# Products by seven in an FFN: which units use them, and where VectorE's differences stand

## The chip, the cores and the metric

The kernel runs on one core of a Trainium2 chip. The metric is the device time of one execution in microseconds, the median of several runs.

## The reference

One decoder block on 256 tokens of width 2048, in float32: two SwiGLU networks around a mixing layer and a cross-attention, each added to the stream h.

```python
h = h + 0.5 * swiglu(rms_norm(h, ffn1_norm), w_gate, w_up, w_down)   # FFN 1: 2048 -> 5632 -> 2048
n = rms_norm(h, mix_norm); P = n @ w_in                              # retention (8 heads) and
h = h + concat(ret, swa) @ w_out                                     # sliding-window attention (16 heads)
h = h + memory_cross_attention(rms_norm(h), rms_norm(mem))           # 4 heads, 256 memory tokens
h = h + 0.5 * swiglu(rms_norm(h, ffn2_norm), ...)                    # FFN 2
out = rms_norm(h, final_norm)
def swiglu(x, w_gate, w_up, w_down):
    return (silu(x @ w_gate) * (x @ w_up)) @ w_down
```

## The kernel before

**A product.** Float32 accuracy is made from three products: each operand is kept as a high part (a rounded copy, made by ScalarE) and a low part (the rest, made by VectorE), and `three` (L664) multiplies high by high, high by low and low by high. The activations stand on the stationary side, 128 tokens at a time; the weights stream in 512 columns. A weight tile `wf` of 128 x 1024 (512 KB) is loaded by a DMA of SyncE's queue into a ring of 11 places, then split: `wh` by ScalarE (L81), `wl` by VectorE (L391), each in a ring of 4. One such tile feeds one step: 2 pieces of the contraction x 2 token halves x 3 = 12 products of 512 columns.

**Units and twins.** A `Unit` is one matrix times 512 columns: 4 blocks of the contraction x 2 steps. A `Twin` joins two matrices (gate and up of the same 512 columns, or two column blocks of a down matrix). Some of its blocks are plain, 4 steps each. A block in `sevens` is done by Strassen's scheme in Winograd's form: 7 half-size products take the place of 8. Each is a chunk, of a kind P1 to P7, with 6 products of 512 columns; so a block costs 42 instead of 48. A chunk's weights are a loaded tile (P1, P3, P5, P2) or a difference of tiles, which `difference` (L244) makes on VectorE in place: P5 is u0 - g0, P6 is u1 - u0, P7 is u1 - g0, P4 is g1 - u1. On the other side stand sums of the activations (`sums_of`, `sums_into` at L302). Each chunk's weights are split like any tile. A chunk's result is combined with the others by copies on ScalarE and additions on VectorE (L265). A unit with two blocks in `sevens` is called here a unit with two groups.

**Order of the work.** FFN units are numbered b = 0 to 10 (512 of the 5632 columns each), in three groups (0 to 3, 4 to 7, 8 to 10); after each group the down product of that group runs. `all_steps` writes one list of steps; the first chunks (P1, P3, P5, P6, P7) of a twin with `ahead` are spread over the steps of the unit before it, P2 and P4 over its own. `run_stream` walks this list: weights are loaded 8 steps and split 3 steps ahead of their products, and `later(n, fn)` issues a task n steps on. The order so written is given to a scheduler, which sets each engine's queue by the data that each instruction needs; tasks keep their place by an explicit dependence (`order`), splits and differences need not. So a difference can stand in VectorE's queue well ahead of the place where it was written.

**Around it.** `cross` (L638) turns a result's layout: VectorE transposes, ScalarE's queue writes to DRAM (`box`), GpSimd's queue reads it back into `t4k`, and a task some steps later (`TURN` = 6 and more) uses it. `Norm.finish` sums the squares of the norm (L593 on VectorE, L596 on TensorE: two products with a column of ones, shown in the profile as four passes) and computes the scale; it is issued `delay` steps after the last square. For the first norm, `n1`, this is early in FFN 1. Twins take their four PSUM banks in turn from two pools, `tmp` (with `spare`) and `acc`. In FFN 1 all units from b = 1 on are twins, with block 2 by seven, and with blocks 2 and 3 for b = 4 and 8 (`DOUBLE`). In FFN 2 it is block 0, and blocks 0 and 1 for b = 4 and 8.

In the mixing stage `rqk_done` rotates q and k (L959 to L963) and `ret_scores` (L972) multiplies them.

Of the kernel before, what the change touches and what calls it, by code (L numbers as in the profile page):

```python
# [43 lines left out]
def decoder_block(ctx: ExitStack, tc: tile.TileContext, a: dict, out: bass.AP):  # L44
# [68 lines left out]
    def later(delay, fn):  # L113
        tasks.append((clock[0] + delay, len(tasks), fn))
# [74 lines left out]
    class Twin:  # L189
# [23 lines left out]
            return self.plain[len(self.plain) - self.late :]  # L213

        def chunks(self, kinds):
            return [
                (self, c, None, kind, c == self.sevens[0], c == self.sevens[-1]) for kind in kinds for c in self.sevens
            ]

        def steps(self):  # L220
            return [
# [16 lines left out]
        def difference(self, b, kind):  # L238
            if kind not in (P5, P6, P7, P4) or (b, kind) in self.made:
                return  # L240
            self.made.add((b, kind))
            g0, g1, u0, u1 = (self.tiles.get((b, f, half)) for f in range(2) for half in range(2))
            dst, p, q = {P5: (u0, u0, g0), P6: (u1, u1, u0), P7: (g0, u1, g0), P4: (u1, g1, u1)}[kind]
            nc.vector.tensor_tensor(dst, p, q, ALU.subtract)  # L244

        def prepare(self, b, kind, between):
            self.difference(b, kind)
# [61 lines left out]
    def sums_of(norm, b, dst, delay, src=None):  # L309

        y = [None]
        src = hT[b] if src is None else src

        def scale():
            y[0] = blk(F32).rearrange("p k c s -> p (k c s)")
            x = y[0][:, :1024].rearrange("p (j k s) -> p j k s", j=2, k=2)
            for k in range(4):
                g = norm.gcol + 4 * b + k
                copy(x[:, k % 2, k // 2, :], src[:, k, :], scale=gains[:, g : g + 1])

        def add():
            x = y[0][:, :1024].rearrange("p (j k s) -> p j k s", j=2, k=2)
            y.append(y[0][:, 1024:].rearrange("p (i j s) -> p i j s", i=4, j=2))
            sums_into(y[1], lambda t, k: x[:, :, k, t * P : (t + 1) * P])

        def part():
            dst[b] = split_sums(y[1])
        for i, fn in enumerate((scale, add, part)):
            later(delay + i, fn)
# [337 lines left out]
    def to_h(w, lhs, factor, blocks, norm=None, then=None, spare=0, seven=None, sums=None, plain=0):  # L667

        def done(s, b):
            if factor != 1.0:  # L670
                y = [t2k() for _ in s]
                for i in range(2):
                    copy(y[i], s[i], scale=factor)
                s = y

            def add(out):
                for t in range(2):
                    v = hT[b][:, :, t * P : (t + 1) * P].rearrange("p q (a j) -> p q a j", a=4)
                    nc.vector.tensor_tensor(v, v, out[t], ALU.add)  # L679
                if norm is not None:  # L680
                    norm.block(b, [hT[b]])
                    norm.stat([hT[b]])
                if then is not None:
                    then(b)
            cross(s, add, TURN + (1 + b // 2 if norm is nmix else spare))
        for b in range(4):
            if seven is None or b < plain:
                Unit(w, b, 512, lhs, lambda acc, b=b: done(acc, b), blocks, pair=True)
            elif b % 2 == 0:
                twin(  # L690
                    [w[2 * i : 2 * i + 2] for i in (b, b + 1)], lhs, [x for x in blocks if x != seven], [seven], sums,
                    lambda f, s, b=b: done(s, b + f),
                )

    twins, input_sums = [], {}

    def twin(*args):

        twins.append(Twin(*args, ahead=bool(twins), spare=len(twins) % 2 == 0))

    def ffn(norm, w_gate, w_up, down, groups, turned):
        gated = {}
        made = {}
        acts = {}

        def gate_done(b, acc):
            assert norm.ready
            gated[b] = [t2k() for _ in range(2)]
            for t in range(2):
                nc.scalar.activation(gated[b][t], acc[t], AF.Silu, scale=norm.scale(t))  # L710

        def up_done(b, acc):
            s = gated.pop(b)
            for t in range(2):
                nc.vector.scalar_tensor_tensor(s[t], acc[t], norm.scale(t), s[t], ALU.mult, ALU.mult)
            turn(b, s)

        def both_done(b, f, acc):
            (gate_done, up_done)[f](b, acc)

        def turn(b, s):

            def made(out):
                acts[b] = blk()
                halves_of(out, parts_of(acts[b]))
                if b in starts:
                    y = blk(F32).rearrange("p k c s -> p (k c s)")[:, :1024].rearrange("p (i j s) -> p i j s", i=4, j=2)
                    sums_into(y, lambda t, k: out[t][:, 2 * k : 2 * k + 2])
                    asums[b] = split_sums(y)
            cross(s, made, TURN + (3 if b < 10 else 1))  # L730

        sums, asums = {}, {}
        twins.clear()
        input_sums[norm] = sums
        starts = [x[0] for x in groups]
        for g, fbs in enumerate(groups):
            for b in fbs:
                done = functools.partial(both_done, b)
                if b > 0:
                    sevens = turned[: 1 + (b in DOUBLE)]  # L740
                    plain = [x for x in range(4) if x not in sevens]
                    twin([w[2 * b : 2 * b + 2] for w in (w_gate, w_up)], norm.blocks, plain, sevens, sums, done)
                    if b == 1:
                        norm.bank = functools.partial(twins[0].bank, 0, 1)
                    continue
                for f, w in enumerate((w_gate, w_up)):
                    Unit(w, b, 512, norm.blocks, functools.partial(done, f), range(4), pair=True)
                if norm is not n1:
                    together(2)
            down(g, acts, fbs, asums)  # L750

# [2 lines left out]
    for b in range(4):  # L754
        if b > 0:
            later(4 * b - 1, lambda b=b: n1.block(b, [hT[b]]))
        later(4 * b + 2 * (b < 3), lambda b=b: n1.stat([hT[b]]))
    for at, b in ((8, 2), (40, 3)):
        later(at, lambda b=b: sums_of(n1, b, input_sums[n1], 0))

    def load_x(b, lo, hi):
        nc.sync.dma_start(hT[b][:, lo:hi, :], a["x"][b * P : (b + 1) * P, lo:hi, :])

    later(24, lambda: nc.sync.dma_start(sinks, a["sinks"]))

    nmix = Norm(G_MIX, "nmix", 3, spread=True)

    def near_mix(b):
        if b == 0:
# [10 lines left out]
            to_h(a["ffn1_w_down"], acts, 0.5, fbs, nmix, near_mix, seven=fbs[0], sums=sums)  # L780
            units[-2].rest = 4

    ffn(n1, a["ffn1_w_gate"], a["ffn1_w_up"], ffn1_down, (range(0, 4), range(4, 8), range(8, 11)), (2, 3))

# [156 lines left out]
    def rqk_done(g, which):  # L943
        def done(acc):
            def finish(out):
                if "rot" not in st:
                    st["rot"] = st["ctab"][:, C_COSR : C_COSR + 512].rearrange("p (c s) -> p c s", c=2)
                    nmix.spread_over(st["rot"])
                if which == 0:
                    st["qk"] = blk(F32)  # L950
                qk = st["qk"]
                for t in range(2):
                    x = out[t]
                    cos, sin = (
                        st["rot"][:, c, t * P : (t + 1) * P].rearrange("p (o a j) -> p o a j", o=1, a=4)
                        .broadcast_to([P, 4, 4, 32]) for c in range(2)
                    )
                    r = squares_of(t2k())
                    nc.vector.tensor_tensor(r[:64], x[64:], sin[64:], ALU.mult)  # L959
                    nc.vector.tensor_tensor(r[64:], x[:64], sin[:64], ALU.mult)  # L960
                    nc.vector.tensor_tensor(x, x, cos, ALU.mult)
                    dst = qk[:, :, which, t * P : (t + 1) * P].rearrange("p q (a j) -> p q a j", a=4)
                    nc.vector.tensor_tensor(dst, x, r, ALU.add)  # L963
                if which == 1:
                    for i in range(4):
                        later(3 + i // 2, lambda i=i: ret_scores(g, i, qk))
            cross(acc, finish, TURN + 2)
        return done

    def ret_scores(g, i, qk):  # L970
        ps = tmp_ps()
        nc.tensor.matmul(ps[:, :S], qk[:, i, 1, :P], qk[:, i, 0, :], start=True, stop=True)  # L972
        nc.tensor.matmul(ps[:, S : S + P], qk[:, i, 1, P:], qk[:, i, 0, P:], start=True, stop=True)
        sT = t2k()
        dm = st["dmat"][g][:, i * S : (i + 1) * S]
        nc.vector.tensor_tensor(sT[:, :S], ps[:, :S], dm, ALU.mult)
        nc.vector.tensor_tensor(sT[:, S : S + P], ps[:, S : S + P], dm[:, :P], ALU.mult)
        st["sT", g, i] = sT
# [375 lines left out]
```

## Time and profile before

| | |
|---|---|
| median of 3 runs | 2144.3 us (2142.32 to 2144.52) |
| the profiled execution | 2140.22 us, of which the span of instructions is 2138.3 us |
| TensorE products busy | 2119.8 us (99%) |
| VectorE busy | 1698.5 us (79%) |
| ScalarE busy | 1236.2 us (58%) |
| GpSimd busy | 161.6 us (8%) |
| DMA | 482.61 MB, 226 GB/s on average |
| TensorE's granted clock, mean | 0.997 |

PE is TensorE's products and PEld its weight loads, DVE is VectorE, ACT ScalarE, POOL GpSimd, SP SyncE. A row of a timeline has the start (us from the span's start), the duration, engine, line, operation and tiles, the count of merged instructions, and in brackets the idle time before it and what ended that. Tile numbers are left out in profiles. A row of a group has the count, the busy time, the mean duration in ns, and the engine's idle time just before these instructions.

### The profile page before, as it was taken

How to read it: one execution, taken by the hardware profiler on the slowest of the kernel's cores; microseconds unless marked ns; L12 is line 12 of the kernel's file. 1: busy time of each engine (PE TensorE's matmuls, PEld its weight loads, DVE VectorE, ACT ScalarE, POOL GpSimd, SP SyncE). 2: the span in 40 equal slices, each digit the busy share in tenths (PEclk: the TensorE clock that was granted, in tenths of full speed). 3: DMA queues.
4: the chain of work that ended last, by engine and by line, in shares of the span. 5: the costliest groups of instructions: out<-in, count | busy, mean ns of one | idle time of the engine just before them, and what ended most of it. 6: DMA issues, size and time to landing. Idle time of an engine off the chain costs nothing.

```text
span 2138.3 us, 26847 instructions
## 1 busy us (share of the span) xinstructions
PE 2119.8 (99%) x9564; PEld 1754.4 (82%) x9564; DVE 1698.5 (79%) x1997; ACT 1236.2 (58%) x1549; POOL 161.6 (8%) x273
## 2 busy tenths in 40 slices
PE   9999999999999999999999999999999999999998
PEld 7888788887888888878888888888888888888886
DVE  7887898778888788777887566578888888888875
ACT  6665565555666664546566454456666556555654
POOL 0000000000100210100101110011010000000000
PEclk9999999999999999999999999999999999999999
DMA  8677787777877876667878875586887677766773
GB/s 301 210 238 217 216 262 235 221 218 220 274 223 233 266 215 203 207 200 241 242 230 234 260 226 186 163 270 216 250 249 244 195 225 218 234 198 208 225 241 113
DMA packets 221286, 482.61 MB, mean 226 GB/s; under 512 B 18144, under 2 KB 18144, under 8 KB 221152
## 3 DMA queue, kind: packets, MB, share of 16 engines
q1 hardware_dynamic: 191312, 413.72, 61.6%
q0 software_dynamic: 12288, 33.57, 7.0%
q10 hardware_dynamic: 17552, 33.60, 4.3%
q8 instruction: 75, 1.23, 0.3%
q14 instruction: 59, 0.48, 0.1%
HBM read 445.17 MB, written 35.65 MB: 225 GB/s over the span
## 4 chain that ended last, share of the span: by engine, by line
PE 89%; DVE 5%; DMA 3%; issue 1%; ACT 1%; POOL 0%; DVEq 0%; ACTq 0%; POOLq 0%; SPq 0%
PE acc L664 55%; PE tmp L664 33%; DVE wl L391 2%; DMA wf<-in_ffn_w_up 1%; DMA wf<-in_ffn_w_gate 1%; DMA wf<-in_xa_wk 1%; ACT wh L81 1%; DVE blk L547 0%; DMA t4k<-box 0%; DMA wf<-in_ffn_w_down 0%; DVE t2k L585 0%; DVE h L679 0%; ACT blk L81 0%; DMA box<-t4k 0%; PE tmp L898 0%
## 5 line engine op out<-in xcount | busy, mean ns | idle before, releaser
L81 ACT ACTIVATE wh<-wf 128x1024 fp32r<-128x1024 f32 (+1 forms) x891 | 933.9, 1054 | 733.5 <-PE acc L664 416.6
L391 DVE TENSOR_TENSOR wl<-wf,wh 128x1024 fp32r<-128x1024 f32 (+1 forms) x886 | 1069.0, 1218 | 349.5 <-ACT wh L81 332.6
L664 PE MATMUL acc<-wh,blk 128*128 128x512 f32 (+1 forms) x3840 | 1211.8, 388 | 1.6 <-ACT wh L81 1.0
L664 PEld LDWEIGHTS acc<-wh,blk 128*128 128x128 f32 x3840 | 719.7, 188 | 151.4 <-ACT wh L81 2.0
L664 PE MATMUL acc<-wl,blk 128*128 128x512 f32 (+1 forms) x1920 | 744.5, 388 | 0.3 <-DVE wl L391 0.3
L664 PE MATMUL tmp<-wh,blk 128*128 128x512 f32 x2232 | 716.7, 390 | 0.0
L664 PEld LDWEIGHTS tmp<-wh,blk 128*128 128x128 f32 x2232 | 419.5, 188 | 87.5 <-ACT t2k L81 0.3
L664 PE MATMUL tmp<-wl,blk 128*128 128x512 f32 x1116 | 435.1, 390 | 2.5 <-DVE wl L391 2.5
L664 PEld LDWEIGHTS acc<-wl,blk 128*128 128x128 f32 x1920 | 361.8, 188 | 73.6 <-DVE wl L391 1.7
L647 POOL DMA_DIRECT2D t4k<-box x256 | 147.8, 584 | 1743.5 <-ACT wh L81 420.3
L664 PEld LDWEIGHTS tmp<-wl,blk 128*128 128x128 f32 x1116 | 209.8, 188 | 47.7 <-DVE wl L391 4.2
L244 DVE TENSOR_TENSOR wf<-wf,wf 128x1024 f32<-128x1024 f32 x152 | 185.9, 1223 | 31.3 <-DMA wf<-in_ffn_w_up 18.5
L81 ACT ACTIVATE t2k<-tmp 128x512 f32<-128x512 f32 x88 | 52.5, 597 | 33.6 <-PE tmp L664 21.1
L638 DVE STREAM_TRANSPOSE t4k<-t2k 128x512 f32<-128x512 f32 x96 | 64.5, 695 | 5.9 <-ACT t2k L81 5.5
L81 ACT ACTIVATE t2k<-acc 128x512 f32<-128x512 f32 x76 | 45.1, 596 | 29.7 <-PE acc L664 15.4
L86 DVE TENSOR_TENSOR blk<-t4k,blk 128x512 fp32r<-128x512 f32 (+2 forms) x72 | 44.3, 655 | 1.3 <-ACT blk L81 0.9
L81 ACT ACTIVATE blk<-t4k 128x512 fp32r<-128x512 f32 (+2 forms) x72 | 39.6, 595 | 3.3 <-DMA t4k<-box 2.6
L81 ACT ACTIVATE blk<-h,gains 128x256 fp32r<-128x256 f32 (+1 forms) x80 | 34.2, 496 | 11.6 <-DVE h L679 9.9
L265 DVE TENSOR_TENSOR tmp<-t2k,tmp 128x512 f32<-128x512 f32 x54 | 35.6, 690 | 0.0
L265 DVE TENSOR_TENSOR acc<-t2k,acc 128x512 f32<-128x512 f32 x48 | 31.7, 689 | 0.0
L547 DVE SCALAR_TENSOR_TENSOR blk<-h,gains,blk 128x256 fp32r<-128x256 f32 x64 | 26.8, 479 | 3.9 <-ACT blk L81 3.7
L679 DVE TENSOR_TENSOR h<-h,t4k 128x512 f32<-128x512 f32 x40 | 25.7, 684 | 2.7 <-DMA t4k<-box 2.7
(141 smaller groups left out, 607.7 us busy)
## 6 DMA issues: line engine op xcount, KB each, us to landing
wf<-in_ffn_w_gate SPq DMA_DIRECT2D x176, 512.0 KB, 5.1
wf<-in_ffn_w_up SPq DMA_DIRECT2D x176, 512.0 KB, 5.0
wf<-in_ffn_w_down SPq DMA_DIRECT2D x176, 512.0 KB, 4.6
box<-t4k ACTq DMA_DIRECT2D x64, 512.0 KB, 5.4
t4k<-box POOLq DMA_DIRECT2D x256, 128.0 KB, 7.1
wf<-in_w_in_rqk SPq DMA_DIRECT2D x32, 512.0 KB, 4.7
wf<-in_w_in_rvg SPq DMA_DIRECT2D x32, 512.0 KB, 4.7
wf<-in_w_out SPq DMA_DIRECT2D x32, 512.0 KB, 5.0
```

Of the source, the lines that this page charges most:

```text
L81: return nc.scalar.activation(dst, src, AF.Copy, **kw)
L86: nc.vector.tensor_tensor(lo, src, hi, ALU.subtract)
L244: nc.vector.tensor_tensor(dst, p, q, ALU.subtract)
L265: nc.vector.tensor_tensor(out, a, b, ALU.add)
L391: nc.vector.tensor_tensor(lo[:, cs], wf[:, cs], hi[:, cs], ALU.subtract)
L547: nc.vector.scalar_tensor_tensor(x[:, k, 1, :], v[:, k, :], g, x[:, k, 0, :], ALU.mult, ALU.subtract)
L638: nc.vector.transpose(z[:, t, :].rearrange("p (g q j) -> p q g j", g=4, q=4), squares_of(v))
L647: nc.gpsimd.dma_start(z[32 * g : 32 * g + 32].rearrange("p t (i n) -> p (t i) n", i=4), far[g])
L664: nc.tensor.matmul(o, x, y, start=first, stop=last, skip_group_check=shared)
L679: nc.vector.tensor_tensor(v, v, out[t], ALU.add)
```

## The change

The parts are these. A difference is tied to the instruction of VectorE that was written just before it, so it can't move ahead of that. In FFN 1 the second unit (b = 1) becomes two plain units, gate and up, and b = 4 and 8 have one group, so only block 2 is ever done by seven, and the sums of block 3 are gone; those of block 2 are made later. In a twin with two groups, which FFN 2 keeps, the chunks of one group come before those of the other, P7 of both last. `ahead` and `spare` are handed over where the count of twins no longer gives what it did. The second norm's statistic is issued one step later, the rotation of q and k one step earlier, with the scores at the same step as before.

```diff
         def chunks(self, kinds):
-            return [
-                (self, c, None, kind, c == self.sevens[0], c == self.sevens[-1]) for kind in kinds for c in self.sevens
-            ]
+            pairs = [(kind, c) for c in self.sevens for kind in kinds if kind != P7]
+            pairs += [(P7, c) for c in self.sevens if P7 in kinds]
+            return [(self, c, None, kind, c == self.sevens[0], c == self.sevens[-1]) for kind, c in pairs]
...
+            last = look()[mybir.EngineType.DVE]
             nc.vector.tensor_tensor(dst, p, q, ALU.subtract)
+            order(last, look()[mybir.EngineType.DVE])
...
-                    lambda f, s, b=b: done(s, b + f),
+                    lambda f, s, b=b: done(s, b + f), **({"spare": True} if plain else {}),
...
-    def twin(*args):
-
-        twins.append(Twin(*args, ahead=bool(twins), spare=len(twins) % 2 == 0))
+    def twin(*args, **kw):
+
+        twins.append(Twin(*args, **{"ahead": bool(twins), "spare": len(twins) % 2 == 0, **kw}))
...
-                if b > 0:
-                    sevens = turned[: 1 + (b in DOUBLE)]
+                if b > (norm is n1):
+                    sevens = turned if b in DOUBLE else turned[:1]
                     plain = [x for x in range(4) if x not in sevens]
-                    twin([w[2 * b : 2 * b + 2] for w in (w_gate, w_up)], norm.blocks, plain, sevens, sums, done)
+                    twin(
+                        [w[2 * b : 2 * b + 2] for w in (w_gate, w_up)], norm.blocks, plain, sevens, sums, done,
+                        ahead=b > 1,
+                    )
...
-                if norm is not n1:
+                if norm is not n1 or b == 1:
                     together(2)
...
-    for at, b in ((8, 2), (40, 3)):
-        later(at, lambda b=b: sums_of(n1, b, input_sums[n1], 0))
+    later(19, lambda: sums_of(n1, 2, input_sums[n1], 0))
...
-    nmix = Norm(G_MIX, "nmix", 3, spread=True)
+    nmix = Norm(G_MIX, "nmix", 4, spread=True)
...
-    ffn(n1, a["ffn1_w_gate"], a["ffn1_w_up"], ffn1_down, (range(0, 4), range(4, 8), range(8, 11)), (2, 3))
+    ffn(n1, a["ffn1_w_gate"], a["ffn1_w_up"], ffn1_down, (range(0, 4), range(4, 8), range(8, 11)), (2,))
...
-                        later(3 + i // 2, lambda i=i: ret_scores(g, i, qk))
-            cross(acc, finish, TURN + 2)
+                        later(4 + i // 2, lambda i=i: ret_scores(g, i, qk))
+            cross(acc, finish, TURN + 1)
```

In the changed kernel some lines have new numbers: L244 (difference) is L245, L391 (split) L393, L593 L595, L596 L598, L598 L600, L664 (product) L666, L679 L681.

What this does to the engines' queues is seen at two places. The first is the statistic of the first norm. VectorE's queue before, in the rows that end with the sum of squares (L593, L598): the `wl` are splits, L547 and L585 the low parts and squares of block 3, L244 a difference of unit 1.

```order
L391 TENSOR_TENSOR wl_59_408<-wf_57_405,wh_58_407 128x1024
L547 SCALAR_TENSOR_TENSOR blk_60_423<-h3_78,gains_79,blk_60_423 128x256 x4
L391 TENSOR_TENSOR wl_63_435<-wf_61_432,wh_62_434 128x1024
L585 TENSOR_TENSOR t2k_24_216<-t2k_24_216,t2k_64_450 128x512
L391 TENSOR_TENSOR wl_68_459<-wf_66_456,wh_67_458 128x1024
L585 TENSOR_TENSOR t2k_24_216<-t2k_24_216,t2k_65_453 128x512
L391 TENSOR_TENSOR wl_78_482<-wf_69_462,wh_77_481 128x1024
L244 TENSOR_TENSOR wf_61_432<-wf_61_432,wf_69_462 128x2x2x256
L391 TENSOR_TENSOR wl_80_498<-wf_70_464,wh_79_497 128x1024
L593 TENSOR_TENSOR t2k_24_216<-t2k_24_216 128x256
L391 TENSOR_TENSOR wl_84_517<-wf_61_432,wh_83_516 128x1024
L598 TENSOR_SCALAR ms_82_513<-tmp_73_469 128x2
```

And VectorE's queue now, at the same place:

```order
L393 TENSOR_TENSOR wl_61_423<-wf_59_420,wh_60_422 128x1024
L587 TENSOR_TENSOR t2k_24_216<-t2k_24_216,t2k_62_438 128x512
L587 TENSOR_TENSOR t2k_24_216<-t2k_24_216,t2k_63_441 128x512
L393 TENSOR_TENSOR wl_66_447<-wf_64_444,wh_65_446 128x1024
L393 TENSOR_TENSOR wl_72_471<-wf_67_450,wh_71_470 128x1024
L595 TENSOR_TENSOR t2k_24_216<-t2k_24_216 128x256
L600 TENSOR_SCALAR ms_75_492<-tmp_74_489 128x2
```

Two splits stand between the last square and the sum (L595), and no difference. On TensorE the two products with ones stood here before, 153 products of 512 columns after the first two steps (11 whole steps of 12, 9 of the next, and two chunks of 6):

```order
L664 MATMUL acc_29_228<-wh_67_458,blk_60_423 128x512
L664 MATMUL acc_29_228<-wl_68_459,blk_60_423 128x512
L664 MATMUL acc_29_228<-wh_67_458,blk_60_423 128x512
L596 MATMUL tmp_73_469<-ones_91,t2k_24_216 128x1 x2
L664 MATMUL acc_29_228<-wh_67_458,blk_60_423 128x512
L664 MATMUL acc_29_228<-wl_68_459,blk_60_423 128x512
```

And now, after 145 of them (12 whole steps and 1 of the next):

```order
L666 MATMUL acc_29_228<-wl_57_396,blk_58_411 128x512
L666 MATMUL acc_29_228<-wh_56_395,blk_58_411 128x512
L666 MATMUL acc_20_160<-wh_60_422,blk_58_411 128x512
L598 MATMUL tmp_74_489<-ones_91,t2k_24_216 128x1 x2
L666 MATMUL acc_20_160<-wl_61_423,blk_58_411 128x512
L666 MATMUL acc_20_160<-wh_60_422,blk_58_411 128x512 x2
```

The last split ahead of the sum (`wl_72`) takes the places of a step whose products end 13 products before this one.

The second place is VectorE's queue in the down product of FFN 1's first group, where unit 4 is prepared. Before, with L679 the addition of a down result to h:

```order
L244 TENSOR_TENSOR wf_407_2097<-wf_407_2097,wf_374_1950 128x2x2x256
L391 TENSOR_TENSOR wl_390_2030<-wf_374_1950,wh_389_2029 128x1024
L391 TENSOR_TENSOR wl_393_2048<-wf_381_1982,wh_392_2047 128x1024
L391 TENSOR_TENSOR wl_396_2060<-wf_385_1998,wh_395_2059 128x1024
L244 TENSOR_TENSOR wf_414_2131<-wf_414_2131,wf_385_1998 128x2x2x256
L391 TENSOR_TENSOR wl_399_2078<-wf_388_2016,wh_398_2077 128x1024
L391 TENSOR_TENSOR wl_406_2094<-wf_391_2033,wh_405_2093 128x1024
L244 TENSOR_TENSOR wf_391_2033<-wf_391_2033,wf_407_2097 128x2x2x256
L244 TENSOR_TENSOR wf_374_1950<-wf_391_2033,wf_374_1950 128x2x2x256
L391 TENSOR_TENSOR wl_409_2112<-wf_394_2051,wh_408_2111 128x1024
L679 TENSOR_TENSOR h0_75<-h0_75,t4k_364_1910 128x4x128 x2
L391 TENSOR_TENSOR wl_413_2128<-wf_397_2063,wh_412_2127 128x1024
```

And now:

```order
L393 TENSOR_TENSOR wl_391_2063<-wf_380_2000,wh_390_2062 128x1024
L681 TENSOR_TENSOR h0_75<-h0_75,t4k_353_1877 128x4x128 x2
L393 TENSOR_TENSOR wl_394_2083<-wf_383_2018,wh_393_2082 128x1024
L245 TENSOR_TENSOR wf_389_2048<-wf_389_2048,wf_374_1965 128x2x2x256
L393 TENSOR_TENSOR wl_402_2101<-wf_386_2036,wh_401_2100 128x1024
L393 TENSOR_TENSOR wl_404_2118<-wf_389_2048,wh_403_2117 128x1024
L681 TENSOR_TENSOR h1_76<-h1_76,t4k_366_1935 128x4x128 x2
L393 TENSOR_TENSOR wl_407_2138<-wf_392_2066,wh_406_2137 128x1024
L245 TENSOR_TENSOR wf_383_2018<-wf_383_2018,wf_389_2048 128x2x2x256
L393 TENSOR_TENSOR wl_410_2150<-wf_395_2086,wh_409_2149 128x1024
L393 TENSOR_TENSOR wl_412_2167<-wf_383_2018,wh_411_2166 128x1024
```

Before, the differences in `wf_407` and `wf_414` each stand 13 rows ahead of the splits that read them, which lie past the rows shown, and two differences follow each other; now each stands two rows ahead of its split (`wf_389` and `wl_404`, `wf_383` and `wl_412`). FFN 2's differences move in the same way.

## The prediction

> **What bounds the kernel now.** I read the page's first part, then the stretches of equal length, then TensorE's waits, and only then the rows around each wait. The first fence has the busy times and TensorE's waits (us in total, times, longest); the second has stretches of 50 us: length, busy time of PE, PEld, DVE, ACT and POOL with instructions in brackets, granted clock, DMA share, GB/s.
>
> ```profile
> PE 2119.8 (99%) x9564; PEld 1754.4 (82%) x9564; DVE 1698.5 (79%) x1997; ACT 1236.2 (58%) x1549; POOL 161.6 (8%) x273
> ...
> PE tmp L596 <- DVE t2k L593: 3.5, 3, 2.2
> PE tmp L664 <- DVE wl L391: 2.5, 4, 0.9
> PE tmp L972 <- DVE blk L963: 0.8, 2, 0.5
> PE acc L664 <- ACT t2k L81: 0.6, 1, 0.6
> ```
>
> ```profile
> 0.00:50.00 50.00, 45.91 (x215) 39.04 (x215) 37.41 (x56) 34.83 (x56) 0.70 (x6) 1.00 0.84 306
> 50.00:100.00 50.00, 49.58 (x206) 40.69 (x207) 40.72 (x45) 28.74 (x34) 4.09 (x5) 0.93 0.69 207
> 100.00:150.00 50.00, 50.00 (x222) 41.42 (x221) 42.52 (x47) 31.85 (x39) 2.30 (x4) 1.00 0.76 228
> ...
> 250.00:300.00 50.00, 48.22 (x210) 39.26 (x211) 45.78 (x46) 28.07 (x31) 4.27 (x8) 1.00 0.76 234
> 300.00:350.00 50.00, 50.00 (x222) 41.40 (x221) 44.87 (x49) 31.43 (x35) 2.63 (x5) 1.00 0.82 238
> ...
> 500.00:550.00 50.00, 48.80 (x213) 39.38 (x212) 44.60 (x45) 28.57 (x32) 3.51 (x7) 1.00 0.76 232
> ...
> 1650.00:1700.00 50.00, 50.00 (x222) 41.40 (x221) 43.30 (x42) 28.44 (x29) 0.00 (x0) 1.00 0.60 190
> ```
>
> TensorE is the bound: busy 99%, and an undisturbed stretch of 50 us holds 222 products, 0.225 us each. So the time is the number of products times this pitch, plus what is lost in a few places: near 50 us (206 products and a granted clock of 0.93), in 250 to 300 (210) and in 500 to 550 (213). The stretch at 1650, in FFN 2, loses nothing. A VectorE that is busy for 44.87 of 50 us at 300 costs nothing either: it hurts only where a split comes late.
>
> The first loss is the largest. Here is TensorE around it, then its products from 51.29 to 58.72 by group, and two stretches of 5 us:
>
> ```profile
> 15.18 0.61 PE L664 MATMUL acc<-wh,blk 128*128 128x512 f32 x2
> 15.63 0.39 PE L664 MATMUL acc<-wl,blk 128*128 128x512 f32 x1
> 15.86 0.61 PE L664 MATMUL acc<-wh,blk 128*128 128x512 f32 x2
> ...
> 47.87 0.40 PE L664 MATMUL acc<-wh,blk 128*128 128x512 f32 x1
> 50.42 1.01 PE L596 MATMUL tmp<-ones,t2k 128*128 128x1 f32 x4 [2.16 <-DVE t2k L593]
> 51.29 0.77 PE L664 MATMUL acc<-wh,blk 128*128 128x512 f32 x1
> ...
> 58.72 0.39 PE L664 MATMUL acc<-wh,blk 128*128 128x512 f32 x1
> ...
> 744.99 0.61 PE L596 MATMUL tmp<-ones,t2k 128*128 128x1 f32 x4 [0.58 <-DVE t2k L593]
> 745.46 0.70 PE L664 MATMUL acc<-wh,blk 128*128 128x512 f32 x2
> ```
>
> ```profile
> L664 PE MATMUL acc<-wh,blk 128*128 128x512 f32 x9 | 4.3, 539 | 0.0
> L664 PE MATMUL acc<-wl,blk 128*128 128x512 f32 x5 | 2.6, 511 | 0.0
> L664 PE MATMUL tmp<-wh,blk 128*128 128x512 f32 x4 | 2.3, 628 | 0.0
> L664 PE MATMUL tmp<-wl,blk 128*128 128x512 f32 x2 | 1.3, 628 | 0.0
> ...
> 50.00:55.00 5.00, 4.58 (x13) 3.81 (x14) 3.67 (x6) 1.12 (x2) 1.62 (x1) 0.54 0.62 206
> 55.00:60.00 5.00, 5.00 (x19) 4.03 (x18) 2.68 (x3) 3.08 (x5) 0.00 (x0) 0.78 0.43 131
> ```
>
> Three products take 15.86 - 15.18 = 0.68 us, so 0.227 each. The product at 47.87 frees TensorE at 48.10; the sum of squares for the first norm (L596) starts at 50.42: 2.3 us lost. Its four one-column passes last 0.87 us until 51.29, against 0.47 at 745: 0.4 lost. From 51.29 to 58.72, 7.43 us, 20 products run instead of 33, under a granted clock of 0.54 and then 0.78: 7.43 - 20 x 0.227 = 2.9 lost. Together 5.6 us.
>
> **The change part by part: the added products.** A group of seven saves 6 products of 512 columns (42 instead of 48). L244, the difference, runs four times for each group:
>
> ```profile
> L244 DVE TENSOR_TENSOR wf<-wf,wf 128x1024 f32<-128x1024 f32 x152 | 185.9, 1223 | 31.3 <-DMA wf<-in_ffn_w_up 18.5
> ```
>
> 152 / 4 = 38 groups. Unit 1 of FFN 1 loses one, units 4 and 8 one each, so 35 stay, and TensorE gets 18 more products: 18 x 0.227 = +4.1 us, bare on the path. VectorE loses 12 differences and 9 splits, ScalarE 9 halves; they had room, and are priced only through the waits.
>
> **The wait of the first norm.** L593 stands in VectorE's queue behind splits and a difference of unit 1's chunks, and the queue is full there. Three rows show the delays: a copy starts when TensorE frees a buffer, the split follows, and L593 comes late.
>
> ```profile
> 27.17 1.06 ACT L81 ACTIVATE wh<-wf 128x1024 fp32r<-128x1024 f32 x1 [1.64 <-PE acc L664]
> 28.26 1.23 DVE L391 TENSOR_TENSOR wl<-wf,wh 128x1024 fp32r<-128x1024 f32 x1 [1.48 <-ACT wh L81]
> ...
> 47.68 1.22 DVE L244 TENSOR_TENSOR wf<-wf,wf 128x1024 f32<-128x1024 f32 x1
> 48.81 1.22 DVE L391 TENSOR_TENSOR wl<-wf,wh 128x1024 fp32r<-128x1024 f32 x1
> 49.95 0.42 DVE L593 TENSOR_TENSOR t2k<-t2k 128x256 f32<-128x256 f32 x1
> ```
>
> Afterwards the order has 145 products of 512 columns ahead of the sum instead of 153, so TensorE arrives 8 x 0.227 = 1.8 us earlier, at 46.28. VectorE's last work before the sum is the split of the step whose buffer comes free 13 products before that, at 43.33. The copy starts then; its split follows 28.26 - 27.17 = 1.09 later and passes the queue on after 49.95 - 48.81 = 1.14, and the sum takes 0.42: ready at 45.98, 0.3 us before TensorE. The wait goes, and with it, I say, the slow spell: -5.6. If a wait as long as before stays, it is 0.
>
> [...]
>
> **Units 4 and 8.** Against 222 products the two stretches lack 12 and 9, at 0.225 us: 2.7 + 2.0 = 4.7 us. The rows:
>
> ```profile
> 248.40 1.23 DVE L244 TENSOR_TENSOR wf<-wf,wf 128x1024 f32<-128x1024 f32 x1 [2.08 <-DMA wf<-in_ffn_w_up]
> 249.54 2.35 DVE L391 TENSOR_TENSOR wl<-wf,wh 128x1024 fp32r<-128x1024 f32 x2
> ...
> 250.82 0.50 PE L664 MATMUL tmp<-wl,blk 128*128 128x512 f32 x1 [0.87 <-DVE wl L391]
> ...
> 505.14 0.50 PE L664 MATMUL tmp<-wl,blk 128*128 128x512 f32 x1 [0.83 <-DVE wl L391]
> ```
>
> A difference that stands six splits or more ahead of the split that needs it waits 2.08 us for its weights, the splits behind it start late, and TensorE waits for them. Both waits lie where a unit with two groups is prepared beside a down product. With the difference kept in program order it stands two rows ahead of its split, and with one group there are three differences and five splits less. What stays for VectorE is what the single units at 300 to 350 have, where nothing is lost. I take -4.7; if the crowding were the down product's own, 0.
>
> **Mixing stage.** The statistic of the second norm is issued one step later: the 0.58 us at 745 go, -0.6. The rotation of q and k is issued one step earlier with the scores where they were, so L972 no longer waits: -0.8. It moves past no late transfer: its tile is read by issues that end at 930.41, a read lands in 7.1 us, and the rotation runs at 952.53, so one step of 12 products, 2.7 us, is there to give. Ends: 0, and -1.4 with the refill that follows each wait.
>
> ```profile
> 928.11 2.30 POOL L647 DMA_DIRECT2D t4k<-box x4 [19.25 <-DMA box<-t4k]
> ...
> 952.53 0.69 DVE L959 TENSOR_TENSOR t2k<-t4k,wf 64x512 f32<-64x512 f32 x1
> ...
> t4k<-box POOLq DMA_DIRECT2D x256, 128.0 KB, 7.1
> ```
>
> **What moves at no cost.** The sums of block 2 now stand late, at unit 2's first chunk, but TensorE reads them only from its second chunk (P3) on, three steps of 2.7 us later, longer than four scaled copies, four differences and one split take; if the chain is late, it is one wait like the 0.87 at 250. The units that take the tmp banks and those that take the acc banks still alternate, one place shifted; a bank that isn't empty yet costs what the one such wait of before did, 0.6 (the row PE acc <- ACT t2k). FFN 2 has the same work: its two units with two groups take the groups one after the other, and its differences stay in order. It loses nothing at 1650, so there is nothing to gain. Differences now lie closer to their use; the three steps (8.2 us) by which splits run ahead cover one that is 1.1 us later: 0, with up to +2 if two units wait like the one at 250.
>
> Sum: 4.1 - 5.6 - 4.7 - 0.6 - 0.8 = -7.6 us against the profiled execution's 2140.2, so 2132.6. Its median of runs is 2144.3, 4.1 higher, and I put the same change on that: **2136.7**.
>
> **Rivals.**
> Slow spell of another origin: the wait goes, the 2.9 + 0.4 stay: -4.3, 2140.0. [...] Against it: the other waits, under 1 us, are followed by a clock of 1.00 (250 to 300), and this one by 0.54. [...]
>
> The waits of units 4 and 8 stay, since a down product's own outputs crowd VectorE: -2.9, 2141.4. Against it: the next units' stretch, 300 to 350, has as busy a VectorE and loses nothing.
>
> The first wait stays: the 0.3 us of room are thin, and a copy or split that comes half a us late brings part of the gap back, at worst all of it: -2.0, 2142.3.
>
> The order itself costs, the case on the other side: a difference kept in place waits for its landing with the next split behind it on VectorE, ScalarE's copy waits for the difference, and TensorE for both. 35 groups have one; a wait of 0.87 us (250.82) in nine of them takes all 7.6 back, and from 14 on the kernel is slower by over 0.2%, about 2149. For it: the 2.08 us at 248.40 are such a wait for weights. Against it: VectorE was idle for 31.3 us in all ahead of its 152 differences, and TensorE's waits for splits came to 2.5.
>
> The order is not kept: the queue printed for the new kernel shows that it is.
>
> **Chances.** Forecast, -10 to -5: 0.70. Slow spell stays 0.08, units 4 and 8 0.08, first wait 0.08 (half of each of these three below 2140, since their prices are for the worst of them), order costs 0.06 (0.04 past the upper bound). 0.2% is 4.3 us, about what a measurement here tells from none: faster means below 2140.0. Faster 0.82, same 0.14, slower 0.04. The range reaches up to the last of the rivals that are still faster, 2142.3, and down to 2132.5: the forecast with 1.4 in the mixing stage, and 3.6 more out of the 18.5 us (2138.3 - 2119.8) that TensorE idles in all.
>
> **What would show it.** Products up by 18; no row at L598 waiting over 0.3 us and a granted clock of 1.00 from 50 to 100; 250 to 300 and 500 to 550 at 222 products; L245 x140, with little idle time for the landing of weights. New waits of TensorE for VectorE's splits in FFN 1 or 2 would prove me wrong.

## The result: 0.55% faster, below the range

The changed kernel takes 2130.9 us (median of 4 runs, 2130.8 to 2131.4), the kernel before in the same comparison 2143.3 (2139.8 to 2144.5): ratio 0.9945, 95% interval 0.9928 to 0.9962. The sign was right; the time lies 1.6 us below the range and 5.8 below the forecast. The profiled execution went from 2140.22 to 2130.97, -9.25 where the sum said -7.6.

The changed kernel's page, first part, then all of TensorE's waits, then VectorE's differences (now L245) as a group:

```profile
PE 2117.3 (99%) x9582; PEld 1754.4 (82%) x9582; DVE 1671.9 (79%) x1967; ACT 1219.7 (57%) x1531; POOL 159.2 (7%) x273
```

```profile
PE acc L666 <- ACT wh L81: 1.4, 2, 1.0
PE tmp L103 <- POOL ident masks.py:199: 1.4, 1, 1.4
PE acc L666 <- DVE wl L86: 0.3, 1, 0.3
```

```profile
L245 DVE TENSOR_TENSOR wf<-wf,wf 128x1024 f32<-128x1024 f32 x140 | 170.5, 1218 | 0.0
```

There are 18 products more, as counted, and TensorE is busy 2.5 us less: before, products that ran under half a clock (0.50 from 50.42 to 57.25; 0.77 us at 51.29) or started behind a wait (0.50 at 250.82) lasted longer than the others (0.39). No wait for a norm's sum or a score product is left, and one of 0.3 for a split. And the row that says most is the last: VectorE was idle for 31.3 us ahead of its differences, 18.5 of them for weights of w_up alone; now for 0.0.

The stretches that were poor before, the one that is poor now, and at the first norm the sum of squares on VectorE and the product with ones on TensorE:

```profile
0.00:50.00 50.00, 47.08 (x227) 39.58 (x228) 33.63 (x50) 32.68 (x52) 1.42 (x7) 1.00 0.94 340
50.00:100.00 50.00, 50.00 (x222) 41.42 (x221) 38.12 (x42) 29.71 (x35) 2.48 (x4) 1.00 0.66 200
...
250.00:300.00 50.00, 50.00 (x223) 41.39 (x222) 41.48 (x42) 28.00 (x32) 4.62 (x8) 1.00 0.79 244
...
500.00:550.00 50.00, 50.00 (x222) 41.40 (x221) 40.32 (x42) 28.22 (x32) 4.63 (x8) 1.00 0.81 245
...
1600.00:1650.00 50.00, 49.62 (x218) 40.47 (x217) 42.26 (x45) 28.12 (x32) 4.62 (x8) 1.00 0.74 236
```

```profile
45.55 0.42 DVE L595 TENSOR_TENSOR t2k<-t2k 128x256 f32<-128x256 f32 x1
...
45.61 0.62 PE L666 MATMUL acc<-wh,blk 128*128 128x512 f32 x2
46.06 0.57 PE L598 MATMUL tmp<-ones,t2k 128*128 128x1 f32 x4
46.49 0.48 PE L666 MATMUL acc<-wl,blk 128*128 128x512 f32 x1
```

The three poor stretches are full, and the product with ones runs without a wait, at 46.06 (46.28 was the estimate). The sum is ready at 45.97 (45.98 was the estimate), so the room is 0.1 us and not the 0.3 of the prediction. One new loss stands at 1608 (218 products), where FFN 2's first down product begins; the kernel before lost nothing there:

```profile
1600.00:1650.00 50.00, 50.00 (x222) 41.40 (x221) 41.20 (x44) 30.35 (x36) 4.60 (x8) 1.00 0.78 237
```

Loss by stage in the two profiled executions, worked out as the distance from each product of 512 columns to the next start, less 0.227 us, summed over stretches of 100 us (a stretch that loses nothing shows -0.1 or -0.2, since the 0.227 is rounded; columns without a loss are left out):

```text
from us      0    200   500   700   800   900  1000  1400  1600   all
before     5.4    2.6   2.0   1.2   3.1   2.3   0.8   0.8  -0.1  17.0
changed    0.0   -0.2  -0.2   0.6   2.2   1.5   0.0   0.1   1.0   4.1
```

That is -12.9, with 4.1 for the products added and -0.4 for the passes with ones at half a clock (0.87 us before, 0.43 now): -9.2, the measured difference.

### The profile page after: what moved, and what is told of

It reads as the page before. It is cut to its first block, busy times and chain, and to the rows that moved or that the text cites. A ratio compares the mean times of both kernels' runs of the same rounds, so it can differ in the third digit from the quotient of the medians.

```text
span 2129.0 us, 26832 instructions
## 1 busy us (share of the span) xinstructions
PE 2117.3 (99%) x9582; PEld 1754.4 (82%) x9582; DVE 1671.9 (79%) x1967; ACT 1219.7 (57%) x1531; POOL 159.2 (7%) x273
## 4 chain that ended last, share of the span: by engine, by line
PE 98%; DVE 1%; issue 0%; DMA 0%; ACT 0%; SPq 0%; ACTq 0%; POOLq 0%; POOL 0%; DVEq 0%
PE acc L666 60%; PE tmp L666 37%; PE tmp L902 0%; DMA h<-in_x 0%; PE tmp L883 0%; PE tmp L849 0%; PE tmp L976 0%; DVE wl L393 0%; PE tmp L598 0%; DVE acc L267 0%; PE tmp L857 0%; PE tmp L997 0%; PE tmp L998 0%; PE tmp L995 0%; PE tmp L977 0%
## 5 line engine op out<-in xcount | busy, mean ns | idle before, releaser
L393 DVE TENSOR_TENSOR wl<-wf,wh 128x1024 fp32r<-128x1024 f32 (+1 forms) x877 | 1063.5, 1219 | 380.4 <-ACT wh L81 346.9
L81 ACT ACTIVATE wh<-wf 128x1024 fp32r<-128x1024 f32 (+1 forms) x882 | 921.6, 1053 | 752.2 <-PE acc L666 366.0
L666 PE MATMUL acc<-wh,blk 128*128 128x512 f32 (+1 forms) x3852 | 1210.9, 387 | 1.4 <-ACT wh L81 1.4
L666 PEld LDWEIGHTS acc<-wh,blk 128*128 128x128 f32 x3852 | 720.0, 188 | 151.9 <-ACT wh L81 3.1
L666 PE MATMUL acc<-wl,blk 128*128 128x512 f32 (+1 forms) x1926 | 745.5, 387 | 0.5 <-DVE wl L86 0.3
L666 PE MATMUL tmp<-wh,blk 128*128 128x512 f32 x2232 | 714.2, 389 | 0.0
L666 PEld LDWEIGHTS tmp<-wh,blk 128*128 128x128 f32 x2232 | 418.9, 188 | 87.6 <-ACT t2k L81 0.4
L666 PE MATMUL tmp<-wl,blk 128*128 128x512 f32 x1116 | 434.2, 389 | 0.0
L666 PEld LDWEIGHTS acc<-wl,blk 128*128 128x128 f32 x1926 | 361.9, 188 | 73.5 <-DVE wl L86 1.1
L666 PEld LDWEIGHTS tmp<-wl,blk 128*128 128x128 f32 x1116 | 209.5, 188 | 43.3
L245 DVE TENSOR_TENSOR wf<-wf,wf 128x1024 f32<-128x1024 f32 x140 | 170.5, 1218 | 0.0
L681 DVE TENSOR_TENSOR h<-h,t4k 128x512 f32<-128x512 f32 x40 | 25.7, 684 | 4.5 <-DMA t4k<-box 4.5
```

Of the source, the lines that this page charges most:

```text
L81: return nc.scalar.activation(dst, src, AF.Copy, **kw)
L393: nc.vector.tensor_tensor(lo[:, cs], wf[:, cs], hi[:, cs], ALU.subtract)
L666: nc.tensor.matmul(o, x, y, start=first, stop=last, skip_group_check=shared)
```

## Experiments

Theory 1: waits near 250 and 500 us come from units with two groups, which crowd VectorE, and fall away with one group. Theory 2: they come from differences that stand early in VectorE's queue and wait for weights, and the tie alone removes them. The runs went in three sets, each with runs of the kernel before, whose medians were 2141.3, 2142.7 and 2141.9. The changed kernel was in none of them, so a difference against its 2130.9 goes from one set to another; that the fastest runs of the kernel before, 2137.3, 2136.9 and 2137.1, agree within 0.4 us speaks for such differences. The ratios are against the kernel before in the same set.

**The kernel before once more** (no edit).

> The kernel before once more, for its spread and the granted clock of each run. Theory 1 (the spread is that of the slow spell after the first norm's wait, which a run has or has not): runs with a mean clock of 0.997 and runs with 0.999, some 3 us apart, and the fastest near 2139. Theory 2 (the spread is that of waits for landing, with the spell in every run): the clock is 0.997 in all runs, while the times spread over 4 to 5 us as they did (2139.8 to 2144.5).

Measured: 2142.0, from 2137.7 to 2144.5. Theory 1 of that expectation is nearer: the time goes with the clock. Over the 64 runs of the kernel before in the three sets, by mean granted clock:

```text
clock   runs   mean us   from     to
0.999     17    2138.7   2136.9   2140.7
0.998     25    2141.7   2137.6   2146.3
0.997     13    2143.5   2140.8   2145.8
0.996      9    2145.3   2141.6   2149.7
```

0.003 of clock is 6.4 us of 2140, and the means differ by 6.6, so the spread goes with the mean clock, by these runs; the lower clock in this kernel's two profiles was 0.50 (from 50.42 to 57.25 in the first). It isn't all of it: at one and the same clock the times still differ by 4 to 9 us, and runs without a profile don't show where their spells and waits lie. The profile of this kernel has the same waits as the first one, with other sizes, and a second spell behind the wait of another norm, FFN 2's:

```profile
PE tmp L596 <- DVE t2k L593: 4.6, 3, 2.1
PE tmp L664 <- DVE wl L391: 3.4, 4, 1.7
```

```profile
1468.46 0.58 PE L596 MATMUL tmp<-ones,t2k 128*128 128x1 f32 x4 [1.48 <-DVE t2k L593]
```

**Without the tie.**

```diff
-            last = look()[mybir.EngineType.DVE]
             nc.vector.tensor_tensor(dst, p, q, ALU.subtract)
-            order(last, look()[mybir.EngineType.DVE])
```

> The changed kernel without the tie that keeps each difference in program order; all else as changed. If the waits near 250 and 500 us went because the units there have one group (crowding), it stays within 1 us of the changed kernel's 2130.9 and TensorE's waits for splits stay away. If they went because no difference stands early in VectorE's queue any more, waits of 0.4 to 0.9 us for splits come back: 2132 to 2136, with a wider spread than the changed kernel's 0.6 us.

Measured: 2153.7 (2148.4 to 2159.6), 0.6% slower than the kernel before (ratio 1.0061, 1.0042 to 1.0081) and 22.8 us slower than the changed kernel. This is far more than either theory said, and it decides for the second: every unit in FFN 1 has one group here. TensorE's waits for splits, the group of differences, and VectorE and TensorE where unit 4 is prepared:

```profile
PE acc L664 <- DVE wl L391: 7.4, 3, 3.8
PE tmp L664 <- DVE wl L391: 6.7, 2, 3.4
...
L244 DVE TENSOR_TENSOR wf<-wf,wf 128x1024 f32<-128x1024 f32 x140 | 171.2, 1223 | 39.6 <-DMA wf<-in_ffn_w_up 30.0 <-DMA wf<-in_xa_wk 4.6 <-DMA wf<-in_xa_wo 1.5
```

```profile
228.75 0.71 DVE L638 STREAM_TRANSPOSE t4k<-t2k 128x512 f32<-128x512 f32 x1 [0.36 <-ACT t2k L81]
234.72 1.23 DVE L244 TENSOR_TENSOR wf<-wf,wf 128x1024 f32<-128x1024 f32 x1 [5.26 <-DMA wf<-in_ffn_w_up]
235.87 1.22 DVE L391 TENSOR_TENSOR wl<-wf,wh 128x1024 fp32r<-128x1024 f32 x1
...
237.14 0.50 PE L664 MATMUL acc<-wl,blk 128*128 128x512 f32 x1 [3.39 <-DVE wl L391]
```

The difference waits 5.26 us for weights that nobody needs yet, the split behind it starts at 235.87, and TensorE has waited 3.39 us when it ends. In VectorE's queue of this kernel that difference stands 17 instructions ahead of its own split, which runs 20.5 us later. In the kernel before, the two that wait 2.08 us at 241.69 and 248.40 stand 14 and 15 ahead; in the changed one every difference stands 2 to 6 ahead, most of them 2.

**Two groups back in units 4 and 8 of FFN 1, with the tie.**

```diff
-    later(19, lambda: sums_of(n1, 2, input_sums[n1], 0))
+    for at, b in ((19, 2), (40, 3)):
+        later(at, lambda b=b: sums_of(n1, b, input_sums[n1], 0))
...
-    ffn(n1, ..., (2,))
+    ffn(n1, ..., (2, 3))
```

> The changed kernel with two groups again in units 4 and 8 of FFN 1 (and the sums of block 3), the tie kept. TensorE has 12 products less, 12 x 0.227 = 2.7 us. If the tie alone took the waits away: 2128.2, faster than the changed kernel. If two groups beside a down product crowd VectorE whatever the order, the 4.5 us of waits come back: about 2132.7.

Measured: 2128.5 (2127.8 to 2129.0), 2.5 us faster than the changed kernel (ratio to the kernel before 0.994, 0.9927 to 0.9953). The stretches:

```profile
250.00:300.00 50.00, 50.00 (x222) 41.18 (x221) 44.59 (x45) 29.98 (x34) 4.60 (x8) 1.00 0.78 242
500.00:550.00 50.00, 50.00 (x222) 41.18 (x221) 44.08 (x45) 29.93 (x33) 4.61 (x8) 1.00 0.79 246
```

VectorE is busy for 44.59 us, near the 45.78 of before, and TensorE misses nothing. With 12 products less and nearly the same loss (4.3 us in all against 4.1), the 2.5 us are those of the products. For units 4 and 8 theory 1 falls: the work was not too much, it stood in the wrong order.

**The second unit of FFN 1 by seven again.**

```diff
-                if b > (norm is n1):
+                if b > 0:
...
-                if norm is not n1 or b == 1:
+                if norm is not n1:
...
-    later(19, lambda: sums_of(n1, 2, input_sums[n1], 0))
+    later(8, lambda: sums_of(n1, 2, input_sums[n1], 0))
```

> The changed kernel with the second unit of FFN 1 by seven again (block 2, one group, its sums at step 8 as before). 6 products less: -1.4 us. If the plain second unit is what took the first norm's wait away, gap and slow spell come back, up to 5.6 us: 2135. If the tie alone is enough (no difference ahead of the sum of squares any more), 2129.5.

Measured: 2131.0 (2130.4 to 2131.4): the same as the changed kernel. The 1.4 us of fewer products are paid back at the norm, by short waits instead of the gap of 2.16 and the slow spell:

```profile
48.70 1.22 DVE L393 TENSOR_TENSOR wl<-wf,wh 128x1024 fp32r<-128x1024 f32 x1
49.83 0.42 DVE L595 TENSOR_TENSOR t2k<-t2k 128x256 f32<-128x256 f32 x1
...
49.97 0.50 PE L666 MATMUL acc<-wl,blk 128*128 128x512 f32 x1 [0.37 <-DVE wl L393]
50.55 0.50 PE L598 MATMUL tmp<-ones,t2k 128*128 128x1 f32 x4
```

**The tie alone**, on the kernel before (the edit is the tie's two lines and nothing else).

> The kernel before with the tie of the differences alone; units, groups, chunk order and mixing stage as before. Theory 1 (the tie is nearly all of the gain): 18 products fewer than the changed kernel (-4.1 us), but about 1.1 us lost at the first norm and 1.4 in the mixing stage: 2127.5 to 2130, faster than the changed kernel. Theory 2 (tie and fewer groups are needed together): 2131 or more, with waits of TensorE for splits near 250 and 500 us.

Measured: 2132.1 (2130.2 to 2135.3) against 2142.7: ratio 0.9954, 0.9937 to 0.9972. The time lies past theory 1's range and at theory 2's, but without the waits near 250 and 500 us that theory 2 asked for. TensorE's waits for splits, and the differences:

```profile
PE acc L666 <- DVE wl L393: 0.9, 2, 0.5
...
L245 DVE TENSOR_TENSOR wf<-wf,wf 128x1024 f32<-128x1024 f32 x152 | 185.0, 1217 | 0.0
```

By the sums per 100 us it loses 2.4 us more than the changed kernel from 700 to 1000, where the estimate had 1.4: the waits at the second norm and the scores, which the mixing stage's part removes. From 1600 to 1700 it loses 0.6 more. So the tie alone gives 10.7 us in this set, where the whole change gave 12.4 in the first.

**Both back: two groups and the unit by seven.** The two edits above together.

> The changed kernel with the second unit of FFN 1 by seven again and two groups in units 4 and 8: of the change only the tie, the order of the chunks group by group and the mixing stage are left. Against the kernel with two groups back (2128.5), 6 products less (-1.4 us), and the wait of about 1.1 us at the first norm that the unit by seven showed: 2128.2. If the two together crowd VectorE, more than 2129.

Measured: 2129.4, but 2127.3 to 2132.6 over the runs. It lies over the 2129 set for crowding, but the loss isn't in the units with two groups: from 200 to 700 the sums per 100 us stay within 0.2 us of the changed kernel's. Its profiled execution, 2131.75, has a wait of 1.43 us at the second norm, probably since a down result landed late, which no run tests (the rows are VectorE's addition to h, and TensorE). Behind it six products of 512 columns take 2.56 us (740.90 to 743.46), 0.43 each instead of 0.227; from 700 to 800 it loses 3.6 us:

```profile
730.10 1.29 DVE L681 TENSOR_TENSOR h<-h,t4k 128x512 f32<-128x512 f32 x2 [2.47 <-DMA t4k<-box]
...
739.31 0.61 PE L598 MATMUL tmp<-ones,t2k 128*128 128x1 f32 x4 [1.43 <-DVE t2k L595]
```

**The mixing stage undone** (the second norm's 4 is 3 again, `TURN + 1` is `TURN + 2`, the scores' 4 is 3).

> The changed kernel with the mixing stage as before: the second norm's statistic one step earlier, the rotation of q and k one step later. By the prediction's term 1.4 us slower, 2132.3, with waits of 0.4 to 0.5 us at each of the two score products and some 0.6 at the second norm. If these waits were only traded for others: 2130.9.

Measured: 2133.3 (2132.7 to 2133.9), 2.35 us slower than the changed kernel; the score products wait 0.8 again (`PE tmp L976 <- DVE blk L967: 0.8, 2, 0.5` in its list of waits). The price was 1.4. By the sums per 100 us it loses 1.9 more than the changed kernel from 700 to 1000; the profiled execution also reached its first product of 512 columns 0.8 us later, at 13.96.

**The old order of chunks** (`pairs` by kind, then by group).

> The changed kernel with the old order of chunks in FFN 2's two units with two groups (each kind for both groups, then the next kind). The prediction put this part at nothing: within 0.7 us of 2130.9. If the old order needs VectorE more densely, the 0.7 us that the changed kernel loses near 1608 us grows to 1.5 to 3.

Measured: 2131.3 (2130.5 to 2132.6): the same, and the loss near 1608 is there too. So the loss isn't the order of the chunks'. VectorE, ScalarE and TensorE of the changed kernel at that place:

```profile
1605.06 1.28 DVE L267 TENSOR_TENSOR acc<-t2k,acc 128x512 f32<-128x512 f32 x2
1606.26 1.21 DVE L245 TENSOR_TENSOR wf<-wf,wf 128x1024 f32<-128x1024 f32 x1
...
1607.59 1.06 ACT L81 ACTIVATE wh<-wf 128x1024 fp32r<-128x1024 f32 x1 [4.97 <-DVE wf L245]
...
1608.70 0.50 PE L666 MATMUL acc<-wh,blk 128*128 128x512 f32 x1 [0.38 <-ACT wh L81]
```

The tied difference waits its turn behind two additions, ScalarE stands still for it, and TensorE loses 0.7 us; neither profile of before loses anything there, and ten of the eleven profiles of kernels with the tie do, that of the tie alone among them. That is the rival on the other side, at one place.

**A gap made on purpose**, first with four additions into a scratch tile ahead of the first norm's sum:

```diff
             x = self.sums
+            if self.gcol == G_FFN1:
+                y = t2k()
+                for _ in range(4):
+                    nc.vector.tensor_tensor(y, x, x, ALU.add)
```

> The changed kernel with four additions of 128 x 512 into a scratch tile on VectorE (about 0.6 us each, 2.4 in all) ahead of the first norm's sum of squares: the gap before the product with ones comes back, about 2.1 to 2.4 us, and nothing else. If the gap causes the slow spell: a granted clock of 0.5 for 3.4 to 7 us right behind it, and 2.4 + 1.7 to 3.4 us more: 2135 to 2137. If the spell had another origin: 2133.3, clock 1.00 at 50 to 60.

Measured: 2131.4 (2131.1 to 2133.9). The scheduler put the product with ones later instead, and no gap came, so this run says nothing on the spell. Then the same with the queues held in program order up to step 16 (`if at in (FIRST, 16): pin()`):

> The changed kernel with four scratch additions of 128 x 512 (2.4 us) ahead of the first norm's sum of squares, and all engines' queues kept in program order up to step 16, so that the product with ones can't move back: TensorE should wait about 2.1 to 2.3 us there. If such a gap causes the slow spell: a granted clock of 0.5 for one or two stretches of 3.4 us behind it and 2134.5 to 2137. If the spell had another origin: a clock of 1.00 and 2133.2.

Measured: 2136.3 (2134.5 to 2137.3). The profiled execution, its fastest, has the gap and no spell. TensorE there, and stretches of 3.41 us of it; below, stretches of the kernel before, and of its second profile:

```profile
49.62 0.61 PE L602 MATMUL tmp<-ones,t2k 128*128 128x1 f32 x4 [2.93 <-DVE t2k L599]
```

```profile
45.22:48.63 3.41, 1.47 (x7) 0.89 (x5) 3.31 (x5) 1.06 (x1) 0.00 (x0) 1.00 0.67 202
48.63:52.05 3.42, 2.43 (x13) 2.10 (x14) 2.21 (x4) 0.00 (x0) 1.54 (x1) 1.00 0.22 82
```

```profile
46.99:50.42 3.43, 1.27 (x6) 0.71 (x5) 3.43 (x5) 1.06 (x1) 0.00 (x0) 1.00 0.51 168
50.42:57.25 6.83, 6.83 (x18) 5.57 (x19) 4.86 (x6) 2.60 (x3) 1.62 (x1) 0.50 0.57 175
```

```profile
1466.09:1469.50 3.41, 1.93 (x11) 1.36 (x11) 3.41 (x6) 1.07 (x2) 0.00 (x0) 1.00 0.44 141
1469.50:1472.91 3.41, 3.41 (x10) 2.67 (x9) 2.29 (x3) 1.55 (x2) 2.76 (x1) 0.50 0.29 91
```

Each spell shown by these stretches has a wait of TensorE beside it: in the kernel before it begins at 50.42, where the wait of 2.16 us ends; in its second profile at 49.55, within the wait of 2.1, and at 1469.50, 1.04 us behind the end of the wait of 1.48. But a wait isn't enough: the 2.93 us in this execution did without (1.00 from 48.63 to 55.46), and so did the 3.39 us in the kernel without the tie (1.00 from 232.07 to 242.30). The other runs of this kernel were up to 2.8 us longer, which a spell like the one of 6.83 us in the kernel before, where 2.9 us were lost, would explain; they have no profile, and their clocks, 0.998 and once 0.997 against 0.998 in the profiled run, don't decide it.

**More units with two groups.** In both FFNs units 4, 6, 8 and 10, on the kernel with two groups back (`DOUBLE = (4, 6, 8, 10)`):

> The changed kernel with two groups in units 4, 6, 8 and 10 of both FFNs: against the kernel with two groups back in units 4 and 8 of FFN 1 (2128.5), 4 x 6 = 24 products less, 24 x 0.227 = 5.4 us. If the tie lets VectorE keep up with two groups in every second unit: 2123.0. If VectorE is crowded by them: TensorE's waits for splits take back 2 to 5 us, 2125 to 2129.

Measured: 2127.6 (2127.0 to 2127.8), ratio to the kernel before 0.9933, 0.9917 to 0.9949: the fastest here, 3.3 us below the changed kernel, but only 0.8 below the kernel with two groups back, where 24 products are worth 5.4. By the same sums per 100 us as above, 1.6 us are lost from 600 to 700, beside FFN 1's last unit and its down product, 0.5 from 300 to 400 and 0.1 to 0.5 in each 100 us from 1700 on: 8.2 us in all against 4.3. The profiled execution also reached its first product of 512 columns 0.7 us later, at 13.9; its first products of 256 columns took 0.41 to 0.47 us from 7.91 to 10.53, and 0.28 from 11.17 on. There are hardly any waits in the list, only late starts, and VectorE is busy for 44.92 of 50 us from 600 to 650, and for 19.82 of 20 from 640 to 660: there it is near its limit. Another kernel has two groups in units 2, 4, 6, 8 and 10 of FFN 2:

> The changed kernel with two groups in units 4 and 8 of FFN 1, and in FFN 2 in units 2, 4, 6, 8 and 10 in place of 4 and 8: 18 products fewer than the kernel with two groups back in FFN 1 (2128.5), -4.1 us: 2124.4 if the tie keeps VectorE out of the way there too. If units with two groups next to each other or to a down product crowd VectorE (for each one about 24 us of splits and differences in 42 us more than a plain unit), waits for splits take it back: 2127 or more.

Measured: 2149.7 (2144.4 to 2151.9). Unit 2 asks for the sums of block 1 before the step at which they were planned; the tasks planned ahead of them are pulled forward, among them the turning of h, so the sums are made of other data than the reference's, and TensorE waits 14.3 us for them. It says nothing on VectorE's load.

## Why the prediction was right and where it was wrong

- **The added products**, +4.1: right; 18 more.
- **The first norm**, -5.6: right in size and for the reason given, fewer splits and no difference ahead of the sum, though with 0.1 us of room. But the plain unit was not needed: by seven and with the tie, the loss there is 1.2 us, for 1.4 saved.
- **Units 4 and 8**, -4.7: right in size, wrong in half of its reason. The text gave the gain to the order and to the single groups together; the single groups cost 2.5 us and bring nothing. Without the tie TensorE loses 18.9 us from 200 to 600, though every unit there has one group.
- **Mixing stage**, -1.4: mis-sized. From 700 to 1000 the loss fell by 2.3; undone, the part costs 2.35 by the medians and 1.9 by these sums. Each of the three waits (0.58 at the second norm, 0.8 in two at the scores) cost about 0.8 us with the late starts behind it, the refill, which the text had only as its other end for the scores.
- **Left out:** the wait of FFN 2's norm near 1460, where 0.8 us went (3.2 lost in the kernel before's second profile, with its spell), and 0.8 from 1000 to 1100, most of it at 1040, behind a difference that waited 6.59 us for weights at 1038.50.
- **FFN 2**, 0: right for the order of chunks; the tie costs 0.7 there at 1608 (1.0 is lost from 1600 to 1700), within the +2 allowed.
- **The step that failed** is the last of the sum: "Its median of runs is 2144.3, 4.1 higher, and I put the same change on that". It took the 4.1 us between one execution and the median of three runs as a fixed offset, and no such offset was there: the changed kernel's median is 2130.9 and its profiled execution 2131.0. Part of the 4.1 was the chance of three runs, since over the 64 runs above the median of the kernel before is 2141.6. The rest goes with waits and spells, more in one run than in another (2136.9 to 2149.7 us, clocks from 0.996 to 0.999), and in its profile the changed kernel has neither at these places; its four runs lie within 0.6 us, at 0.999 each time. How much of each run's time is which stays open without their profiles. This step is 4.1 of the 5.8 us by which the forecast was off. The other 1.6 are terms of the sum, which said 2132.6 for the profiled execution: in the main 0.9 more in the mixing stage and 1.6 in the two places left out, less the 1.0 lost from 1600 to 1700.
- **The rivals.** The price of the order on the other side was thought to be a wait in each of many groups; it came at one place. The spell was gone with the gap in the profiled execution of the changed kernel, and the clock was 0.999 in all four runs. That the spell goes with the wait was the author's estimate, and the runs show it in part: in the kernel before the half clock began at 50.42, at the end of the wait of 2.16 us, and TensorE had been busy for 1.27 of the 3.43 us before; but the gap made on purpose, 2.93 us, had a clock of 1.00 behind it. The spells that the stretches show lasted 6.83 us, and 3.41 at 1469.50 in the second profile of the kernel before.

## What to carry to other kernels

An instruction that a scheduler moves ahead in an engine's queue, because its inputs should be there by then, holds up what stands behind it when a transfer lands late: here one waited 5.26 us, and the split behind it began only when it had run. Idle time of an engine ahead of one kind of instruction, ended by transfers, is the sign (31.3 us before, 0.0 after), and a tie to the place where it was written cost little here, 0.7 us at one place. A stage with an engine 90% busy and waits behind it need not be crowded: look first at what stands at the head of the queue. And the distance between one profiled execution and the median of a few runs is no property of the kernel: where the times of a kernel differ by several us from run to run and its clock with them, a change that removes waits can take that distance away too, and many runs with their clocks are needed to place the median.

## What was not expected of the hardware

A longer wait did not always bring the half clock, and a shorter one could. Its spells, with TensorE's wait beside each: 0.50 from 50.42 to 57.25 in the kernel before, at the end of a wait of 2.16 us; in its second profile 0.50 from 49.55 to 56.38, begun within a wait of 2.1, and from 1469.50 to 1472.91, 1.04 us behind the end of a wait of 1.48; in the kernel without the tie 0.50 from 283.27 to 286.69, behind 3.41 us of which TensorE was busy for 0.37. Two waits without one: 2.93 us in the gap made on purpose, with 1.00 from 45.22 to 55.46, and 3.39 us in the kernel without the tie, ended at 237.14, with 1.00 from 232.07 to 242.30. So 1.48 us had a half clock behind it and 3.39 had none; the length of one wait doesn't decide it in these profiles, and what does was not shown by any run.
